# Gate matrix of the dense block made between the stages of the last block, and every gather paced by a weight unit

## The chip, the cores and the metric

The kernel runs on one core of a Trainium2 chip, as one program of five engines (PE for matmuls, DVE, ACT and POOL for the rest, SP for issuing plain transfers) that each work through their own list of instructions in order and wait for each other through semaphores. The metric is device time in microseconds; the number that counts is the median of a few runs.

## The reference, cut to what matters

One decoder layer for 1024 tokens of width 1024. Three token mixers (a state-space branch, a gated spatial branch, cross-attention to 256 memory rows) are merged and projected; then comes a channel mixer with 16384 single-neuron experts, of which each token takes 8 heads x 16.

```
def block(xt):                                   # PEER, 128 tokens
    q = (xt @ w_peer_q).reshape(t, HEADS, 2, HALF)
    sc = einsum('thid,hikd->thik', q, peer_keys)     # scores against 128 + 128 keys
    top_v, top_i = top_k(sc, 16)
    cand, cidx = sums of all pairs (i, j), index i * 128 + j
    best_v, best_pos = top_k(cand, 16); eid = cidx[best_pos]
    gate = softmax(best_v)
    act = gelu(einsum('thkd,td->thk', peer_u[eid], xt))
    return einsum('thk,thkd->td', gate * act, peer_v[eid])
x = x + peer_ffn(rms_norm(x)); return rms_norm(x)
```

## The kernel before

The tokens are handled in three blocks of 256, 512 and 256 (`BLOCKS`). Each block goes through `mixer` (projections, branches, output projection) and then `routing` (scores, top 16, gates). The mixer of a block is a generator: it hands back labels such as "conv", "chunk", "gap", "attended", and the caller puts other work at these places. So the routing of block 0 stands beside the first convolutions of block 1, and the routing of block 1 beside those of block 2; the routing of block 2 has no mixer beside it.

The expert layer is done in two ways. Blocks 0 and 2 (512 tokens, four tiles `tt` of 128) **gather**: for each of the 128 slots of a token tile, `rows_of` (L804) has POOL issue an indirect transfer of 128 rows of 4 KB from `u`; DVE multiplies it with the token rows and sums (L821, into a column of the tile `dots`); after a gelu the same is done with rows of `v`, which DVE adds up in PSUM (L828). That makes 1024 gathers of 512 KB. They land in `NG` = 7 buffers with the tags `g40` to `g46`, slot k in buffer k mod 7. The middle block (`DENSE`) computes all experts densely: `dense_act` (L943) makes an activation tile of 128 experts, a "uT" unit; `gate_matrix` (L832) writes the gates as a dense matrix to memory (`g_d`); `dense` (L865) multiplies both and runs the product through all of `v`.

A **unit** (L170) is 512 KB of weights: a load, a rounded copy `whi` by ACT (L163) and the remainder `wlo` by POOL or DVE (L164). Each product is then three matmuls (L190 to L192). 64 of the 128 activation tiles are made early and stored (`fill`, `act_d`): three at each head of the routing of block 1, two at each chunk and gap of the mixer of block 2, two at each head of its routing.

`gate_matrix` works on 4 tokens at a time, a "quad", 128 of them: two one-hot matrices by DVE (L847), a scaling by POOL (L851) and ACT (L854), four matmuls of 128x128 (L857), and a copy by ACT into a stage tile of 2 MB (L859), which is stored after every 8 quads (L861). It stands alone between the last routing and the dense stage, with 8 uT units beside it.

The order of instructions on every engine is set when the program is built, by a scheduler that goes by a priority (`tc.cur_priority`) and by its own estimate of when operands and buffers are ready. Buffers of one tag are handed out in the order in which the code asks for them, and the code of the gathers is the last to ask (L1059). `pace` gives a gather the priority of a weight unit, so that it stands behind that unit: the first ones behind units of the first routing, those from 300 (`NPRE`) on behind units of the dense stage. Between these, pace returns nothing and the scheduler places the gathers where it finds room.

## Time and profile before

| what | value |
|---|---|
| median of three runs | 3782.76 us (3782.18 to 3792.6) |
| the profiled execution | 3768.97 us, of which the span of its instructions is 3767.2 us |
| busy: PE, DVE, POOL, ACT | 87%, 77%, 67%, 39% |
| granted PE clock, mean | 0.938 |
| read and written in HBM | 953.95 MB and 72.35 MB |

All stage times below are of the profiled execution. The stages overlap at their ends, since each engine passes from one to the next by itself; the cuts used here are where DVE begins and ends a routing, and where PE begins the dense stage and DVE ends it. The share of busy time is a mean over stages with different limits.

### The profile page before, as it was taken

The page shows a single profiled execution, that of the slowest core. Times are in us where ns is not written, and L with a number is a line of the kernel's source. Part 1 is how long each engine was busy: PE and PEld are TensorE (multiplying, and loading weights), DVE is VectorE, ACT ScalarE, POOL GpSimd, SP SyncE. Part 2 cuts the span into 40 slices and gives each one's busy share as a digit, 9 for nine tenths or more (in the row PEclk, how much of TensorE's full clock was granted, in tenths as well). Part 3 has the DMA queues.
Part 4 walks back from the last instruction along what each step waited for, and adds up shares of the span by engine and source line. Part 5 has one row for each costly group of instructions (what it writes and reads, how often), then busy time and mean ns, then how long its engine had stood idle before and what let it go on. Part 6 is the DMA issues. An engine that isn't in the chain of part 4 may idle for free.

```text
span 3767.2 us, 49553 instructions
## 1 busy us (share of the span) xinstructions
PE 3292.5 (87%) x16928; PEld 2774.3 (74%) x16928; DVE 2910.4 (77%) x5391; ACT 1485.9 (39%) x2212; POOL 2527.5 (67%) x1860
## 2 busy tenths in 40 slices
PE   7899979889999888883999986488899999999995
PEld 6799867768877677763788875377777778777774
DVE  2532479998888899999741389967679988887988
ACT  5554544434223345432354443276322223222221
POOL 6577756777787666666876667655456666665665
PEclk9999999999999899986999998698999999999998
DMA  5355555789999988777965577744899999998997
GB/s 194 101 166 188 202 189 201 264 321 340 339 355 339 336 303 278 250 242 260 360 222 166 182 250 250 276 175 194 304 327 362 329 350 344 352 343 311 357 330 281
DMA packets 362653, 1029.61 MB, mean 273 GB/s; under 512 B 33568, under 2 KB 118944, under 8 KB 359968
## 3 DMA queue, kind: packets, MB, share of 16 engines
q0 software_dynamic: 147456, 536.94, 39.5%
q1 hardware_dynamic: 214944, 489.50, 37.8%
q8 instruction: 134, 2.20, 0.2%
q14 instruction: 119, 0.97, 0.1%
HBM read 953.95 MB, written 72.35 MB: 272 GB/s over the span
## 4 chain that ended last, share of the span: by engine, by line
PE 35%; DVE 22%; issue 8%; POOL 5%; ACT 3%; DMA 2%; POOLq 0%; DVEq 0%; ACTq 0%; SPq 0%
PE mm_ps L191 9%; PE mm_ps L192 9%; PE mm_ps L190 9%; DVE g L821 5%; DVE row_ps L828 3%; POOL g L811 2%; PE tp_ps L192 2%; PE tp_ps L190 2%; PE tp_ps L191 2%; POOL wlo L164 2%; PE mm_ps L857 1%; DVE d L847 1%; DVE wlo L164 1%; DMA g<-in_v_dram,eid 1%; ACT a L859 1%
## 5 line engine op out<-in xcount | busy, mean ns | idle before, releaser
L164 POOL TENSOR_TENSOR wlo<-raw,whi 128x1024 fp32r<-128x1024 f32 x484 | 1162.1, 2404 | 423.9 <-ACT whi L163 396.8
L163 ACT CAST whi<-raw 128x1024 fp32r<-128x1024 f32 (+1 forms) x623 | 648.0, 1044 | 1095.0 <-PE mm_ps L191 329.8
L190 PE MATMUL mm_ps<-a,whi 128*128 128x512 f32 (+1 forms) x2744 | 947.6, 349 | 113.6 <-ACT whi L163 42.9
L192 PE MATMUL mm_ps<-a,wlo 128*128 128x256 f32 (+1 forms) x2744 | 937.3, 344 | 33.1 <-DVE wlo L164 19.6
L191 PE MATMUL mm_ps<-a,whi 128*128 128x512 f32 (+1 forms) x2744 | 941.2, 343 | 1.1 <-DVE a L164 0.9
L811 POOL DMA_INDIRECT g<-in_v_dram,eid x512 | 537.8, 1050 | 361.8 <-DVE row_ps L828 212.2
L811 POOL DMA_INDIRECT g<-in_u_dram,eid x512 | 528.6, 1032 | 326.5 <-DVE g L821 158.4
L828 DVE SCALAR_TENSOR_TENSOR row_ps<-g,dots,row_ps 128x1024 f32<-128x1024 f32 x512 | 656.5, 1282 | 21.0 <-DMA g<-in_v_dram,eid 14.6
L190 PEld LDWEIGHTS mm_ps<-a,whi 128*128 128x128 f32 x2744 | 534.2, 195 | 182.6 <-ACT whi L163 49.6
L821 DVE SCALAR_TENSOR_TENSOR g<-g,row_ps 128x1024 f32<-128x1024 f32 x512 | 608.5, 1208 | 40.5 <-DMA g<-in_u_dram,eid 40.2
L192 PEld LDWEIGHTS mm_ps<-a,wlo 128*128 128x128 f32 x2744 | 533.2, 195 | 94.8 <-DVE wlo L164 21.6
L191 PEld LDWEIGHTS mm_ps<-a,whi 128*128 128x128 f32 x2744 | 535.4, 195 | 56.6 <-DVE a L164 2.1
L191 PE MATMUL mm_ps<-wlo,d 128*128 128x512 f32 x1024 | 410.2, 401 | 5.3 <-POOL wlo L164 4.6
L192 PE MATMUL mm_ps<-whi,d 128*128 128x512 f32 x1024 | 406.2, 399 | 0.0
L190 PE MATMUL mm_ps<-whi,d 128*128 128x512 f32 x1024 | 375.7, 399 | 20.7 <-ACT d L163 8.7
L190 PEld LDWEIGHTS mm_ps<-whi,d 128*128 128x128 f32 x1024 | 193.2, 189 | 73.1 <-ACT whi L163 9.7
L164 DVE TENSOR_TENSOR wlo<-raw,whi 128x1024 fp32r<-128x1024 f32 x139 | 194.6, 1400 | 58.0 <-ACT whi L163 57.0
L191 PEld LDWEIGHTS mm_ps<-wlo,d 128*128 128x128 f32 x1024 | 195.2, 191 | 55.9 <-POOL wlo L164 8.0
L192 PEld LDWEIGHTS mm_ps<-whi,d 128*128 128x128 f32 x1024 | 194.9, 190 | 46.5
L857 PE MATMUL mm_ps<-d,d 128*128 128x128 f32 x1024 | 156.6, 315 | 55.6 <-POOL d L851 39.4
L857 PEld LDWEIGHTS mm_ps<-d,d 128*128 128x128 f32 x1024 | 143.8, 223 | 69.0 <-POOL d L851 54.9
L847 DVE TENSOR_TENSOR d<-iota,tp_ps 128x512 bf16<-128x512 f32 (+1 forms) x256 | 155.5, 678 | 36.9 <-ACT tr L839 24.8
(311 smaller groups left out, 5052.7 us busy)
## 6 DMA issues: line engine op xcount, KB each, us to landing
raw<-in_win_a_dram SPq DMA_DIRECT2D x156, 512.0 KB, 4.2
raw<-in_uT_a_dram SPq DMA_DIRECT2D x128, 512.0 KB, 5.3
raw<-in_v_b_dram SPq DMA_DIRECT2D x128, 512.0 KB, 6.7
raw<-in_br_a_dram SPq DMA_DIRECT2D x72, 512.0 KB, 3.9
g_d<-a SPq DMA_DIRECT2D x16, 2048.0 KB, 6.3
a<-g_d SPq DMA_DIRECT2D x32, 1024.0 KB, 10.7
raw<-in_win_b_dram SPq DMA_DIRECT2D x48, 512.0 KB, 4.9
raw<-in_pq_a_dram SPq DMA_DIRECT2D x48, 512.0 KB, 3.6
```

The lines of the kernel that those rows point to most:

```text
L163: return (nc.scalar.copy(hi, src), (eng or nc.vector).tensor_tensor(lo, src, hi.bitcast(F32), op=ALU.subtract))
L164: (eng or nc.vector).tensor_tensor(lo, src, hi.bitcast(F32), op=ALU.subtract))
L190: nc.tensor.matmul(ps, lhsT=l_hi, rhs=r_hi, start=start, stop=False)
L191: nc.tensor.matmul(ps, lhsT=l_hi, rhs=r_lo, start=False, stop=False)
L192: nc.tensor.matmul(ps, lhsT=l_lo, rhs=r_hi, start=False, stop=stop)
L811: nc.gpsimd.indirect_dma_start(out=g, out_offset=None, in_=a[table], in_offset=bass.IndirectOffsetOnAxis(ap=eid[:, k:k + 1], axis=0))
L821: nc.vector.scalar_tensor_tensor(g, g, 1.0, xn, op0=ALU.mult, op1=ALU.mult, accum_out=col(w, k))
L828: nc.vector.scalar_tensor_tensor(acc, g, col(w, k), acc, op0=ALU.mult, op1=ALU.add)
L847: nc.vector.tensor_tensor(one_hot, iota[:, None, :].to_broadcast([P, 4, P]), tp[:, n * P + m0:n * P + m0 + 4, None].to_broadcast([P, 4, P] ...
L857: nc.tensor.matmul(ps[:, u * P:(u + 1) * P], lhsT=oj[:, u, :], rhs=oi[:, u, :], start=True, stop=True)
L859: nc.scalar.copy(stage[:, :, q * 4:q * 4 + 4].rearrange("p i t -> p t i"), ps.rearrange("p (t i) -> p t i", t=4))
```

## The change

The gate matrix becomes a generator that hands back after every quad. It is asked for 8 quads (one stage tile) at each "gap" of the last block's mixer, and the branches and the spatial loop get more gaps (26 in all instead of 10). Its one-hot tiles no longer come from the dense stage's pool: both f32 matrices of a quad lie in a gather buffer, one of `g44` to `g46`, and the stage tile is a `b16` buffer of the mixer. The stored activation tiles are 56 instead of 64, made at other places: 2 at each head of the routing of block 1, one at each gap once the gate matrix is done, 3 at each head of the last routing, the rest after it. `pace` now has a unit for every gather: units of the routings and mixers carry rates (`RATE_ROUTING`, `RATE_MIXER`, `RATE_LAST`), and what is left is spread over the dense units. While the gate matrix is made, gathers are to use four buffers (`slots`). 30% of the remainders of the dense stage's units go to DVE, before 50%.

```diff
-NPRE = 300
-RATE_ROUTING = 0.5
-ACT_SPILL = 64
-FILL_ROUTING = (3, 2)
-FILL_GAP = 2
+RATE_ROUTING, RATE_MIXER = (1.0, 0.3), (1.5, 0.5)
+RATE_LAST = 0.5
+ACT_SPILL = 56
+FILL_ROUTING = (2, 3)
+NQ_GATHER = 4
+QUADS_GAP = 8
-LO_MIXER, LO_DENSE = 0.34, 0.5
+LO_MIXER, LO_DENSE = 0.34, 0.3
...
-            g = gat.tile([P, D], F32, tag=f"g4{k % NG}", name="g4", bufs=1)
+            g = gat.tile([P, D], F32, tag=f"g4{k % slots(n)}", name="g4", bufs=1)
...
-            stage = a16().rearrange("p (i t) -> p i t", t=STG)
+                stage = b16().rearrange("p (i t) -> p i t", t=STG)
...
+                    quad = gat.tile([P, D], F32, tag=f"g4{NQ_GATHER + nq[0] % (NG - NQ_GATHER)}", name="quad", bufs=1)
...
-        rate[0] = 0
+        rate[0] = RATE_MIXER[b - 1]
         now = nxt
...
-            if held_xT:
-                fill(FILL_GAP)
+    m_gate = len(marks)
+    quads = gate_matrix(ij_dense, gate_dense)
+    gates_done = False
     for label in now:
         if label == "gap":
-            fill(FILL_GAP)
+            for _ in range(QUADS_GAP):
+                if next(quads, 0) == 0:
+                    gates_done = True
+            if gates_done:
+                fill(1)
+        elif label == "attended":
+            for _ in quads:
+                pass
...
+    m_gathers = len(marks)
+    rate[0] = RATE_LAST
     routing(xnT, b16()[:, 0:2048], gate[:, 2:4], eid[:, 2:4], beside=lambda: fill(FILL_ROUTING[1]))
...
-    for t in range(TT):
-        gate_matrix(t, ij_dense, gate_dense, dp, beside_gates)
+    fill(len(todo), dp)
+    acts = [dense_act(i, held_xT[0], dp, None, mm_ps()) for i in range(AHEAD)]
+    rate[0] = 0
...
-        if n < NPRE:
-            return None
-        return units[min(int((n - NPRE) * len(units) / (TT * SLOTS - NPRE)) + lag, len(units) - 1)]
+        return units[min(int((n - n1) * len(units) / (TT * SLOTS - n1)) + lag, len(units) - 1)]
+
+    def slots(n):
+
+        shared = n < n1 and m_gate <= at[bisect_right(due, n) - 1] < m_gathers
+        return NQ_GATHER if shared else NG
```

The built order of instructions shows at three places what this moves. A row names a line of its own kernel; lines of the changed kernel are up to 14 higher. First POOL in the first routing, before; the DMA rows are gathers, and consecutive slots have names three apart:

```order
L760 TENSOR_TENSOR b_4673<-b_4673,topi 128x512
L811 DMA g_27932<-in_u_dram,eid 128x1024
L811 DMA g_27935<-in_u_dram,eid 128x1024
L811 DMA g_27938<-in_u_dram,eid 128x1024
L811 DMA g_27941<-in_u_dram,eid 128x1024
L811 DMA g_27944<-in_u_dram,eid 128x1024
L811 DMA g_27947<-in_u_dram,eid 128x1024
L811 DMA g_27950<-in_u_dram,eid 128x1024
L164 TENSOR_TENSOR wlo<-raw,whi 128x1024
L811 DMA g_27953<-in_u_dram,eid 128x1024
```

The same place on POOL in the changed kernel:

```order
L769 TENSOR_TENSOR b_4673<-b_4673,topi 128x512
L820 DMA g_27648<-in_u_dram,eid 128x1024
L820 DMA g_27651<-in_u_dram,eid 128x1024
L820 DMA g_27654<-in_u_dram,eid 128x1024
L820 DMA g_27657<-in_u_dram,eid 128x1024
L165 TENSOR_TENSOR wlo<-raw,whi 128x1024
L820 DMA g_27669<-in_u_dram,eid 128x1024
L165 TENSOR_TENSOR wlo<-raw,whi 128x1024
L820 DMA g_27672<-in_u_dram,eid 128x1024
L820 DMA g_27675<-in_u_dram,eid 128x1024
L165 TENSOR_TENSOR wlo<-raw,whi 128x1024
L820 DMA g_27678<-in_u_dram,eid 128x1024
```

Slots 0 to 3 and 7 to 10 (buffers `g40` to `g43`) stand here; slots 4, 5 and 6 do not. The next gather on POOL stands in the mixer of block 2, behind the last scaling of a quad (L864):

```order
L864 TENSOR_TENSOR quad<-quad,tr 128x384 x8
L529 TENSOR_TENSOR b_10218<-b_10218,t_16541 128x256
L165 TENSOR_TENSOR wlo<-raw,whi 128x1024
L529 TENSOR_TENSOR b_10218<-b_10218,t_16576 128x256
L165 TENSOR_TENSOR wlo<-raw,whi 128x1024
L864 TENSOR_TENSOR quad<-quad,tr 128x384 x5
L820 DMA g_27666<-in_u_dram,eid 128x1024
L820 DMA g_27660<-in_u_dram,eid 128x1024
L820 DMA g_27663<-in_u_dram,eid 128x1024
```

By DVE's products with gathered rows, 4 of 1024 stand ahead of the last one-hot matrix; before, 576 stood ahead of the first. The second place is DVE at the end of the dense stage, in the kernel before (L940 is the last step of the dense stage, L828 a product with a gathered row):

```order
L828 SCALAR_TENSOR_TENSOR row_ps<-g_31061,dots,row_ps 128x1024
L940 SCALAR_TENSOR_TENSOR a_21046<-a_21046,rs_r,row 128x1024 x4
L828 SCALAR_TENSOR_TENSOR row_ps<-g_31064,dots,row_ps 128x1024
...
L828 SCALAR_TENSOR_TENSOR row_ps<-g_31091,dots,row_ps 128x1024
L148 TENSOR_SCALAR rs_v<-ssf 128x1
```

And in the changed kernel (L945 adds a dense result, L830 and L837 are the products with gathered rows):

```order
L945 TENSOR_TENSOR a_20514<-a_20514,mm_ps 128x512
L830 SCALAR_TENSOR_TENSOR g_29498,dots<-g_29498,row_ps 128x1024
...
L954 SCALAR_TENSOR_TENSOR a_20514<-a_20514,rs_r,row 128x1024 x4
L830 SCALAR_TENSOR_TENSOR g_29534,dots<-g_29534,row_ps 128x1024
...
L837 SCALAR_TENSOR_TENSOR row_ps<-g_30807,dots,row_ps 128x1024
L149 TENSOR_SCALAR rs_v<-ssf 128x1
```

Behind the last addition of a dense result stood 18 such products, and now stand 426 (45 slots of `u` and 128 of `v` for the third tile, 128 and 128 for the fourth; 3 of them wait in the pipeline). On POOL 429 gathers follow the last weight unit. The third place is ACT at the stage tile's first copy, with the semaphores that each row waits for (DMAHW is a plain transfer). Before, in the gate matrix:

```order
L859 COPY a_19412<-mm_ps 128x4x128 [waits PE_49] x2
L163 CAST whi<-raw 128x1024 [waits DMAHW2_49,PE_49]
L946 ACTIVATE d_19549<-mm_ps 128x512 [waits PE_49]
L839 COPY tr<-tp_ps 128x128 [waits PE_49]
...
L859 COPY a_19559<-mm_ps 128x4x128 [waits DMAHW7_49,PE_49]
```

And in the changed kernel, in the mixer of block 2, where L164 is the rounded copy of a weight unit:

```order
L872 COPY b_14641<-mm_ps 128x4x128 [waits PE_49]
L867 ACTIVATE quad<-quad,tr 128x128 [waits DVE_49,Pool_49]
L164 CAST whi<-raw 128x1024 [waits PE_49]
L867 ACTIVATE quad<-quad,tr 128x128 [waits DVE_49] x2
L164 CAST whi<-raw 128x1024 [waits DMAHW0_49,PE_49]
L164 CAST whi<-raw 128x1024 [waits DMAHW1_49,PE_49]
L867 ACTIVATE quad<-quad,tr 128x128 [waits DVE_49]
L872 COPY b_14807<-mm_ps 128x4x128 [waits DMAHW0_49]
```

Before, that wait is for the store of the tile before the last one (two tiles take turns). Now it is for the store of the tile just filled: one buffer serves all 16.

## Rows read from the trace of the kernel before

**Rows 1.** Windows, one for each stage; after the engines granted clock, DMA share, GB/s

```profile
0.00:484.00 484.00, 430.52 (x2931) 394.49 (x2932) 180.50 (x315) 257.38 (x419) 330.08 (x171) 0.97 0.51 168
484.00:743.00 259.00, 224.38 (x1177) 191.38 (x1176) 229.66 (x772) 119.02 (x175) 181.97 (x139) 0.93 0.65 222
743.00:1316.00 573.00, 530.22 (x2418) 426.57 (x2417) 499.17 (x655) 200.40 (x332) 433.68 (x347) 0.96 0.93 338
1316.00:1756.00 440.00, 327.88 (x1696) 280.37 (x1693) 436.54 (x1271) 178.78 (x235) 292.76 (x220) 0.86 0.78 265
1756.00:2170.00 414.00, 383.96 (x2237) 334.68 (x2238) 195.98 (x219) 187.65 (x275) 310.25 (x184) 0.97 0.69 238
2170.00:2388.00 218.00, 154.03 (x832) 133.49 (x831) 206.12 (x686) 73.25 (x105) 154.22 (x124) 0.87 0.75 254
2388.00:2674.00 286.00, 207.64 (x1252) 184.65 (x1252) 209.05 (x357) 170.97 (x279) 158.25 (x174) 0.82 0.55 210
2674.00:3731.00 1057.00, 1033.87 (x4392) 828.71 (x4392) 923.04 (x1090) 294.90 (x388) 654.57 (x493) 0.99 0.94 338
3731.00:3767.00 36.00, 0.00 (x0) 0.00 (x0) 30.34 (x37) 3.53 (x7) 11.76 (x12) 0.55 0.69 260
```

**Rows 2.** Windows of the gathers on POOL alone (L811): busy us and count

```profile
743.00:1316.00 573.00, 264.17 (x258) 0.96 0.93 338
2674.00:3731.00 1057.00, 436.74 (x403) 0.99 0.94 338
```

**Rows 3.** Windows of DVE's products, second routing: L821 (two instructions each), then L828

```profile
1316.00:1756.00 440.00, 87.08 (x146) 0.86 0.78 265
1316.00:1756.00 440.00, 82.73 (x65) 0.86 0.78 265
```

**Rows 4.** The page's line of POOL's remainders; the dense stage on its own (window as rows 1)

```profile
L164 POOL TENSOR_TENSOR wlo<-raw,whi 128x1024 fp32r<-128x1024 f32 x484 | 1162.1, 2404 | 423.9 <-ACT whi L163 396.8
...
2750.00:3650.00 900.00, 881.39 (x3751) 706.25 (x3750) 786.83 (x919) 251.24 (x323) 561.80 (x421) 0.99 0.95 340
```

**Rows 5.** The last block's mixer in two parts (windows, columns as in rows 1)

```profile
1800.00:2000.00 200.00, 184.16 (x1071) 159.23 (x1070) 112.16 (x115) 90.17 (x123) 160.21 (x101) 0.98 0.80 278
2000.00:2170.00 170.00, 165.79 (x973) 145.94 (x972) 44.37 (x63) 79.41 (x120) 113.21 (x58) 1.00 0.52 172
```

**Rows 6.** Lines of the gate matrix, ns min/median/max; its store's landing; its matmuls in order

```profile
L859 ACT COPY a<-mm_ps x128: 1023/1084/1267, 2406.2 to 2652.8; 128x512 f32<-128x512 f32 x128
L854 ACT ACTIVATE d<-d,tr x128: 377/402/470, 2402.9 to 2651.7; 128x128 f32<-128x128 bf16 x128
DMA to landing us min/median/max: 6.2/6.3/12.2
2542.12 10.85 PE L857 MATMUL mm_ps<-d,d 128*128 128x128 f32 x78 [3.79 <-POOL d L851]
```

**Rows 7.** The page: the gathers' queue, and loads of remembered keys and values

```profile
q0 software_dynamic: 147456, 536.94, 39.5%
b<-kv_d SPq DMA_DIRECT2D x2, 2048.0 KB, 10.5
```

**Rows 8.** Gathers close together: start, us; DVE, then POOL; then a window

```profile
3746.22 13.21 DVE L828 SCALAR_TENSOR_TENSOR row_ps<-g,dots,row_ps 128x1024 f32<-128x1024 f32 x10
2396.57 0.94 POOL L811 DMA_INDIRECT g<-in_u_dram,eid  x1 [0.30 <-issue]
2397.82 0.94 POOL L811 DMA_INDIRECT g<-in_u_dram,eid  x1 [0.30 <-issue]
2425.00:2435.00 10.00, 4.15 (x16) 3.56 (x16) 10.00 (x18) 2.82 (x6) 6.96 (x8) 0.50 0.95 340
```

**Rows 9.** From one token tile to the next on DVE, in the dense stage

```profile
3108.50 1.27 DVE L828 SCALAR_TENSOR_TENSOR row_ps<-g,dots,row_ps 128x1024 f32<-128x1024 f32 x1
3124.65 1.21 DVE L821 SCALAR_TENSOR_TENSOR g<-g,row_ps 128x1024 f32<-128x1024 f32 x1
```

**Rows 10.** Landing of the gathers (all 1024)

```profile
DMA to landing us min/median/max: 4.0/6.8/12.5
```

More of the change, by code (lines that the diff above doesn't have):

```diff
@@ L519, in branch @@
             for f in range(KD):
+                if f % 2:
+                    yield "gap"
                 sg = gate(n, f)
@@ L526, in branch @@
                     nc.gpsimd.tensor_tensor(merged[:, f, :], merged[:, f, :], sg, op=ALU.add)
-        branch(0, yT)
+        yield from branch(0, yT)
         ss = sml.tile([P, TT], F32, tag="ss", name="ss")
@@ L553, in mixer @@
         for g in range(8):
+            if g % 2:
+                yield "gap"
             ug, wsp = ug_next, wsp_next
@@ L568, in mixer @@
             split(yT[0][:, g, :], yT[1][:, g, :], m1)
-        branch(1, yT)
-        kv = a16() if compact else b16()
+        yield from branch(1, yT)
+        kv = b16()
         nc.sync.dma_start(kv, kv_d)
@@ L607, in turn_probs @@
         def turn_probs(prs):
-            pT = [tp_ps()[:, :T], tp_ps()[:, :T]]
+            if compact:
+                both = tp_ps()
+                pT = [both[:, 0:T], both[:, T:2 * T]]
+            else:
+                pT = [tp_ps()[:, :T], tp_ps()[:, :T]]
             for t in range(TT):
@@ L639, in mixer @@
         nc.sync.dma_start(x2, x_d[t0:t0 + T, :].rearrange("(t p) d -> p t d", p=P))
-        branch(2, yT)
+        yield from branch(2, yT)
         yield "gap"
@@ L800, in held, with gathered @@
         return ps
-    def gathered(tt, eid, gt, pace):
+    def gathered(tt, eid, gt, pace, slots):
         def rows_of(table, k, half):
@@ L1044, in layer_kernel @@
     units = marks[m_dense:m_last]
-    early_units = [m for m in marks if m[3] > 0]
+    at = [n for n, m in enumerate(marks) if m[3] > 0]
+    early_units = [marks[n] for n in at]
     due, total = [], 0.0
@@ L1054, in pace @@
             return early_units[bisect_right(due, min(n + lag * .5, due[-1])) - 1]
-        if n < NPRE:
-            return None
-        return units[min(int((n - NPRE) * len(units) / (TT * SLOTS - NPRE)) + lag, len(units) - 1)]
+        return units[min(int((n - n1) * len(units) / (TT * SLOTS - n1)) + lag, len(units) - 1)]
+    def slots(n):
+        shared = n < n1 and m_gate <= at[bisect_right(due, n) - 1] < m_gathers
+        return NQ_GATHER if shared else NG
     for t in range(TT):
-        gathered(t, eid[:, t], gate[:, t], pace)
+        gathered(t, eid[:, t], gate[:, t], pace, slots)
 _OUTS = [((1, 1024, 1024), 'float32')]
```

75 lines of the change are left out of this document (36 added, 39 removed).

## The prediction

> **What bounds the kernel now.** I read the windows cut by stage first [rows 1], since the means of the page hide that the stages have different limits. PE is the limit in the projections at the start, in both large mixers and above all in the dense stage (1033.87 of 1057 us, clock 0.99). DVE is the limit in the routings: 436.54 of 440 us in the second, 206.12 of 218 us in the third. The stage between 2388 and 2674 us, in which the gate matrix is made, has no engine over 73% busy and costs 286 us; that is what the change goes after. The gathers are filler: 258 of 1024 are issued in the mixer of block 1 and 403 in the dense stage [rows 2]. In the second routing their products cost DVE 87.08 + 82.73 = 170 of its 440 us [rows 3]. At the end, 18 products stand behind the dense stage, and the kernel ends 36 us after it.
>
> **The change: what it does to the gathers.** This decides the forecast. The quads now live in `g44` to `g46`, and they ask for these buffers earlier in the code than any gather does. A gather of slot 4, 5 or 6 therefore comes after the last quads, and the products of one tile, which all write `dots`, stand in order: after slot 3 nothing goes on. The built order shows it: 8 gathers in the first routing, none in the mixer of block 1 and the second routing, the ninth behind the last quad. The rates for these units have no effect. From there to the dense stage some 180 are issued, in the dense stage 408 (now 403), and 426 products are left behind it. An engine's order can't be changed by the chip, so this remainder is certain; only its pace is open.
>
> **Part by part.** From row to row of [rows 1], in us:
>
> 1. *Start, 484*: nothing moves, 484.
>
> 2. *First routing and mixer of block 1, 259 + 573 = 832.* 4 products with gathered rows instead of some 310 leave DVE mostly idle. PE was busy for 224.38 + 530.22 = 755, so no more than 77 can come back. DVE was not what PE waited for in the mixer (573 - 530 = 43 of idle in all, 499 busy on DVE), and in the routing DVE's own 230 - 70 remain in a chain; I take 24 off: **808** (755 to 832).
>
> 3. *Second routing, 440.* Without its gathers DVE has 436.54 - 170 = 267 left. PE has 327.88 less 8 uT units. A unit is 24 matmuls of 900 / 3751 = 0.240 us [rows 4], 5.76 us, so 8 are 46 us: 282 left. Neither engine fills such a stage alone when both are needed for each head; at the 88% that DVE and PE reach in the first routing (230 and 224 of 259) PE's 282 becomes **320** (282 to 400), 120 less.
>
> 4. *Mixer of block 2, 414.* Until 1800 nothing changes (44). The quads lie between there and some 2000. PE gains 128 x 8 matmuls of 10.85 / 78 = 0.139 us, 142 us [rows 6], and loses about 12 uT units, 69 us: 184 + 142 - 69 = 257, now 184 [rows 5]. But ACT has a floor of its own. The stage tile has one buffer, where two took turns. Each of 16 tiles needs 8 copies of 1.084, 8 scalings of 0.402 and the store's 6.3 before the next can begin [rows 6], 8.7 + 3.2 + 6.3 = 18.2, and 16 of them 291 us. Behind a copy that waits for the store stand the rounded copies of the next weight units, and PE waits for these. I take a little over that floor, 310 for the 200 (260 to 360). POOL's scaling of f32 in place is not in the trace; by its remainders, 2404 ns for 1024 f32 elements [rows 4], 384 take 0.90, 115 us in all. POOL would then have about 310 - 56 + 115 + 88 - 31 = 426 of 575 (less early gathers, plus scalings and backlog, less 13 units), so no cost; between nothing and twice that it stays under the sum. Then the backlog starts: some 85 gathers before 2170, where there were none. A gather takes the 16 DMA engines 0.395 x 3767 / 1024 = 1.45 us [rows 7], 123 us, on top of 0.52 x 170 = 88 [rows 5]: 211 for 170, so I take 213 (165 to 225), set by transfers. The keys and values of the memory need the buffer of the last stage tile and come 6.3 + 10.5 us after its filling [rows 6, 7], in part under two queries: 8 (0 to 17). Sum 44 + 310 + 213 + 8 = **575** (470 to 650).
>
> 5. *Third routing, 218.* DVE does the same with 61 gathers for 62. PE has 8 units more, 154 + 46 = 200 of 218. **226** (215 to 245).
>
> 6. *Gate stage, 286.* Left are 6 + 8 uT units, 14 x 5.76 = 81, of which a few start under the routing. **75** (60 to 105).
>
> 7. *Dense stage, 1057.* 64 activations instead of 56: 8 x 5.76 = 46, with PE at 98% and as many gathers as before. POOL does 135 remainders instead of 92, 43 x 2.40 = 103 us more on 655 [rows 1, 4], still under 72%. **1103** (1085 to 1140).
>
> The dense stage then ends at 484 + 808 + 320 + 575 + 226 + 75 + 1103 = 3591, against 3731: the moved gate matrix alone is worth 140 us.
>
> 8. *The remainder, 36 now.* 426 gathers with nothing beside them. POOL can issue one every 2397.82 - 2396.57 = 1.25 us; DVE takes 87.08 / 73 = 1.19 for a row of `u` [rows 3] and 13.21 / 10 = 1.32 for one of `v` [rows 8]. From 2425 to 2435 gathers alone moved 340 GB/s at a DMA share of 0.95 [rows 8], so 524,288 bytes each take 1.54 us; the mean over the run is 1.45. I take 1.50 (1.25 to 1.67, the last by the dearest of these with a tenth on it): 639 us. Three changes from `u` to `v` or tile to tile follow; each has 3124.65 - 3109.77 = 15 us without a product [rows 9], of which the filled buffers give back some: 12 each, 36. The last tile's norm and store need 8, as now. **683** (570 to 770).
>
> Span: 3591 + 683 = 4274. The profiled execution lies 2 us above its span and the median of the runs 14 above that; I say 4280, 13% slower.
>
> **The rivals.**
>
> *The remainder goes at DVE's pace.* If transfers keep up, 173 rows of `u` at 1.25 (POOL's pace, DVE's being shorter) and 253 of `v` at 1.32 take 550 instead of 639: about 4190. For it: 7 buffers and a median landing of 6.8 us [rows 10], taken under load, allow one gather in about 1.2 us. Against: the window at 340 GB/s had POOL issuing without a wait for DVE in most of its gathers and still did not reach that. The Trainium skill (DMA: Bandwidth & Descriptors, Anatomy of one DMA) gives a transfer from POOL 2.0 us and its bytes at 436 GB/s; by that page's figures seven in flight would never be the limit, and this rival would hold. No row here shows gathers quite alone.
>
> *The last mixer chokes.* If the single stage tile stops ACT in every one of 16 rounds for a store that takes the 12.2 us of the worst row [rows 6] instead of 6.3, that is 16 x 6 = 94 more: 4370. For it: POOL's and SP's transfers share the same 16 engines, and weights are loaded at the same time. Against: the backlog has not begun there, and DMA was at 0.80 with gathers that are now gone.
>
> *The change does what it says.* If gathers did run early and only a remainder like now's stayed, the end would be at 3591 + 36 = 3627, a good 4% **faster**. It would need gathers ahead of the quads on POOL; the order has 8. The point from which it turns: the 140 us gained before the end pay for 140 / 1.5 = some 90 gathers more in the remainder, and there are 408 more.
>
> **How the numbers follow.** Forecast 4280: 0.62. DVE's pace, 4190: 0.18. Choked mixer, 4370: 0.15. As intended, 3627: 0.04. Something that cancels out to no change: 0.01. The first three are all slower. The range takes in the terms' bounds around the forecast, not all at one end at once: for stages 2 to 7 some 80 to either side, for the remainder 90, and the two rivals lie within; 4130 to 4410. About 0.3% is what a measurement of this kernel can tell from no change: faster 0.04, same 0.01, slower 0.95.
>
> **What would show it.** Right: in the slices, 600 us or more at the end with PE at 0 and DMA near 0.95; no gather on POOL from some 550 us until the gate matrix is done; DVE half empty in the second routing, which shrinks by about 120 us; the stage tile's first copies waiting for a store; the first dense product near 2490 and the last near 3590. Wrong: gathers in the mixer of block 1; a remainder at under 1.3 us a gather; a mixer of block 2 that takes no longer than before, so that the end comes nearer to 4150.

## The result, and the profile after

The changed kernel takes 4090.66 us (4087.09 to 4092.4) where the kernel before takes 3782.47 (medians of four runs each, one more of the kernel before than above); the ratio is 1.081 [1.0795, 1.0825]. Slower was right, and the place was right: a remainder of 425 products behind the dense stage. The time is 189 us below the forecast and 39 below its range. The profiled execution has a span of 4090.7 us.

The slices of the page after (engine, then busy tenths in 40 equal slices of 102 us):

```profile
PE   7899999999999998888788999999999999000000
DVE  3532576432439985666699788887888878898889
PEclk9999999999999999999899999999999999555555
DMA  5254453234233344569977999989999998999998
GB/s 193 99 200 160 164 175 118 78 111 141 96 127 135 132 135 165 207 223 350 348 267 251 326 326 335 334 308 335 326 325 330 332 334 316 370 396 363 376 369 349
```

The last six slices are the remainder: no work on PE, its granted clock at 0.5, the DMA engines full. In the middle, from the seventh slice to the fifteenth, the reverse: DMA at 0.2 to 0.4 while PE is at 0.9. These are the stages in which the gathers used to run.

Windows of the changed kernel, cut at the same events as [rows 1] (us; PE, weight loads, DVE, ACT, POOL busy and count; granted clock, DMA share, GB/s). The starting stage now ends at 492 because I cut it at DVE's first maximum; in the kernel before that event also lies at 492.

```profile
0.00:492.00 492.00, 438.61 (x2998) 402.57 (x2999) 182.59 (x316) 259.60 (x424) 332.29 (x173) 0.97 0.48 166
492.00:690.00 198.00, 191.20 (x1033) 162.48 (x1032) 147.39 (x661) 110.20 (x149) 119.10 (x80) 0.99 0.43 151
690.00:1224.00 534.00, 522.15 (x2506) 427.32 (x2505) 201.88 (x270) 201.82 (x347) 191.28 (x96) 1.00 0.31 108
1224.00:1490.00 266.00, 255.23 (x1446) 221.99 (x1444) 263.64 (x1053) 147.02 (x192) 128.18 (x71) 0.98 0.40 136
1490.00:2043.00 553.00, 463.77 (x3062) 420.33 (x3062) 361.10 (x580) 321.70 (x520) 416.50 (x333) 0.94 0.67 247
2043.00:2280.00 237.00, 200.54 (x975) 169.04 (x974) 230.80 (x683) 81.00 (x117) 167.49 (x129) 0.91 0.79 268
2280.00:2358.00 78.00, 72.28 (x310) 58.73 (x309) 54.46 (x47) 21.90 (x31) 65.14 (x48) 0.98 0.93 330
2358.00:3481.00 1123.00, 1089.61 (x4608) 872.80 (x4608) 942.04 (x1129) 315.43 (x411) 769.48 (x552) 0.99 0.92 327
3481.00:4091.00 610.00, 0.00 (x0) 0.00 (x0) 546.39 (x623) 12.97 (x19) 393.92 (x420) 0.50 0.96 371
```

And the gathers on POOL alone (one line of the kernel, by window):

```profile
492.00:690.00 198.00, 7.78 (x8) 0.99 0.43 151
690.00:1490.00 800.00, 0.00 (x0) 0.99 0.34 118
...
3481.00:4091.00 610.00, 393.92 (x420) 0.50 0.96 371
```

Eight gathers, then none for 800 us, where [rows 2] had 258 in the mixer of block 1 alone. Stage by stage, forecast against measured: first routing and mixer of block 1, 808 (counted from 484) against 732 (from 492), which puts their end at 1292 and 1224; second routing 320 against 266; mixer of block 2, 575 against 553; third routing 226 against 237; gate stage 75 against 78; dense stage 1103 against 1123; remainder 683 against 610. So the dense stage ended at 3481 and not 3591. Three terms carry the miss: 68 us in the first, 54 in the second routing, 73 in the remainder.

### The profile page after: what moved, and what is told of

Same layout as the page of the kernel before. It is cut to its first block, busy times and chain, and to the rows that moved or that the text cites. A ratio compares the mean times of both kernels' runs of the same rounds, so it can differ in the third digit from the quotient of the medians.

```text
span 4090.7 us, 49506 instructions
## 1 busy us (share of the span) xinstructions
PE 3233.4 (79%) x16928; PEld 2735.3 (67%) x16928; DVE 2930.3 (72%) x5354; ACT 1471.6 (36%) x2201; POOL 2583.4 (63%) x1897
## 5 line engine op out<-in xcount | busy, mean ns | idle before, releaser
L165 POOL TENSOR_TENSOR wlo<-raw,whi 128x1024 fp32r<-128x1024 f32 x521 | 1258.6, 2421 | 591.0 <-ACT whi L164 536.9
L164 ACT CAST whi<-raw 128x1024 fp32r<-128x1024 f32 (+1 forms) x623 | 647.5, 1044 | 1012.0 <-PE mm_ps L193 366.9
L191 PE MATMUL mm_ps<-a,whi 128*128 128x256 f32 (+1 forms) x2808 | 946.7, 340 | 24.6 <-ACT whi L164 12.9
L192 PE MATMUL mm_ps<-a,whi 128*128 128x256 f32 (+1 forms) x2808 | 942.9, 337 | 1.0 <-DVE a L165 0.9
L820 POOL DMA_INDIRECT g<-in_u_dram,eid x512 | 509.8, 996 | 306.8 <-DVE g L830 162.4
L837 DVE SCALAR_TENSOR_TENSOR row_ps<-g,dots,row_ps 128x1024 f32<-128x1024 f32 x512 | 658.9, 1287 | 47.1 <-DMA g<-in_v_dram,eid 31.9
L820 POOL DMA_INDIRECT g<-in_v_dram,eid x512 | 509.9, 996 | 283.8 <-DVE row_ps L837 142.0
L830 DVE SCALAR_TENSOR_TENSOR g<-g,row_ps 128x1024 f32<-128x1024 f32 x512 | 610.9, 1214 | 63.3 <-DMA g<-in_u_dram,eid 49.0
L191 PEld LDWEIGHTS mm_ps<-a,whi 128*128 128x128 f32 x2808 | 539.7, 193 | 82.6 <-ACT whi L164 16.2
L192 PEld LDWEIGHTS mm_ps<-a,whi 128*128 128x128 f32 x2808 | 540.9, 193 | 53.3 <-DVE a L165 1.6
L165 DVE TENSOR_TENSOR wlo<-raw,whi 128x1024 fp32r<-128x1024 f32 (+1 forms) x102 | 151.6, 1486 | 116.3 <-ACT whi L164 111.5
L191 PE MATMUL tp_ps<-a,whi 128*128 128x512 f32 x512 | 200.9, 392 | 5.5 <-ACT whi L164 5.5
L193 PE MATMUL tp_ps<-a,wlo 128*128 128x512 f32 x512 | 201.3, 393 | 2.0 <-POOL wlo L165 2.0
L192 PE MATMUL tp_ps<-a,whi 128*128 128x512 f32 x512 | 200.6, 392 | 0.0
```

Of the source, the lines that this page charges most:

```text
L164: return (nc.scalar.copy(hi, src), (eng or nc.vector).tensor_tensor(lo, src, hi.bitcast(F32), op=ALU.subtract))
L165: (eng or nc.vector).tensor_tensor(lo, src, hi.bitcast(F32), op=ALU.subtract))
L191: nc.tensor.matmul(ps, lhsT=l_hi, rhs=r_hi, start=start, stop=False)
L192: nc.tensor.matmul(ps, lhsT=l_hi, rhs=r_lo, start=False, stop=False)
L193: nc.tensor.matmul(ps, lhsT=l_lo, rhs=r_hi, start=False, stop=stop)
L820: nc.gpsimd.indirect_dma_start(out=g, out_offset=None, in_=a[table], in_offset=bass.IndirectOffsetOnAxis(ap=eid[:, k:k + 1], axis=0))
```

## The experiments

Theory: gathers stop because the quads ask first for buffers that later slots need; the remainder is the bill. Rivals: the pacing behind weight units holds them back, or the remainder is only an effect of a slower middle. Three further questions are about sizes: why the middle was so much shorter, what sets the remainder's pace, and what sets the 310 us of the quads (from the first one-hot matrix to the last, on DVE).

Runs 3 and 4 were measured five and four times, all others once. How much a stage varies without a change in it can be seen in runs 6 to 8, which differ from the changed kernel in the remainder alone: there the quads took 311, 317 and 314 us where the changed kernel has 310, and the dense stage 1114 to 1116 where it has 1123. Smaller differences are not read as effects.

**1. Four buffers until the last mixer ends.** The gathers keep out of the quads' buffers; the pacing is untouched.

```diff
-        shared = n < n1 and m_gate <= at[bisect_right(due, n) - 1] < m_gathers
+        shared = n < n1 and at[bisect_right(due, n) - 1] < m_gathers
```

> The changed kernel, with the gathers using four buffers (g40 to g43) in all units up to the end of the last mixer, not only while the gate matrix is made. Theory (gathers are held because the quads ask for g44 to g46 first): the gathers now start in the first routing and run through the mixer of block 1, 260 of them. There they stop again, since the last step of token tile 0 asks for g46 (its result tile), behind the quads. So some 200 products stay behind the dense stage instead of 425: at 1.40 us 315 us less there, some 60 us more in the first routing and mixer (DVE busy again), in all about 3840 us. Rival (the pacing rates alone put the gathers late): no gather before the quads, 4090 us as now.

Measured 3836.92. 64 gathers ran in the first routing and 196 in the mixer of block 1; then they stopped again, because the result tile of the first token tile asks for a buffer of the quads (`fin` in `g46`). 199 products stood behind the dense stage, which was followed by 287 us instead of 610. One line on buffers takes 254 us off, with the pacing as it was: it is the buffers that hold the gathers, and not the pacing.

**2. The result tile in the fourth buffer too.** As run 1, and:

```diff
-        out = gat.tile([P, D], F32, tag=f"g4{NG - 1}", name="fin", bufs=1)
+        out = gat.tile([P, D], F32, tag=f"g4{NQ_GATHER - 1}", name="fin", bufs=1)
```

> The changed kernel; until the last mixer's end the gathers use four buffers that no quad asks for, as in the run e1, and the result tile of the products sits in the fourth of them instead of one that the quads hold. Nothing is left out. The order then has 51 gathers in the first routing, 219 in the mixer of block 1, 72 in the second routing and 121 behind the dense stage (e1: 64, 196, 0 and about 193). Theory, a gather in the second routing costs DVE's 1.18 us, one in the mixer of block 1 some 0.15, one in the remainder 1.37: 78 fewer in the remainder give back 107, 72 in the second routing cost 85, 23 more in the mixer 3: about 3815 (3800 to 3825) against 3837 of e1. Rival, a gather taken out of the remainder is all gain: about 3735.

Measured 3836.41, the same as run 1, though 75 fewer products were left. The remainder took 178 us, 109 less, as expected. The second routing took 342 instead of 265 us with its 57 gathers, the mixer of block 1 597 instead of 583. Missing from both theories was what happened among the quads: 43 gathers stand there, where run 1 has none, and the stretch took 380 instead of 316 us, 1.5 us for each gather. From the quads to the end of the dense stage 48 us came back; no run was made on that. The window of the quads in run 2 (columns as above):

```profile
1724.00:2104.00 380.00, 297.76 (x1944) 277.86 (x1944) 263.60 (x410) 230.40 (x356) 261.39 (x234) 0.86 0.60 218
```

**3. Gathers asked for ahead of the quads, in all seven buffers.** The gathers' function becomes a generator that is driven up to the gate matrix's place in the code, so that the early gathers get their buffers first.

```diff
         for k in range(SLOTS):
+            yield tt * SLOTS + k / 2
             g, m1 = rows_of("u", k, 0)
...
         for k in range(SLOTS):
+            yield tt * SLOTS + (SLOTS + k) / 2
             g, _ = rows_of("v", k, 1)
...
     m_gate = len(marks)
+    so_far, prio = sum(m[3] for m in marks) - 2, tc.cur_priority
+    for n in asked:
+        if n >= so_far:
+            break
+    tc.cur_priority = prio
     quads = gate_matrix(ij_dense, gate_dense)
...
```

> The changed kernel, with the gathers whose units lie ahead of the gate matrix asked for in the code ahead of the quads (344 of them), with all seven buffers; rates, quads and everything else stay. Theory: with the order of the requests put right the gathers flow as the rates say, 480 ahead of the dense stage, 121 behind its last unit (the built order). Stages: 492 + 790 + 290 + 560 + 237 + 70 + 1123 = 3562, then 121 x 1.38 + 25 = 192: about 3755 us, no more than 1% from the kernel before. The clock in the second routing falls below 0.98, as DVE fills up. Rival (something else in the change costs the time, such as the single stage buffer or the added gaps): it stays above 3950 us.

Measured 3769.19 (3768.57 to 3772.55), ratio 0.9958 [0.9944, 0.9973]: a little faster than before, and 14 slower than expected. The gathers run where the change meant them to (81, 230 and 37 in the first three stages behind the start), and 121 products are left.

**4. The same, with more gathers in the routings.** As run 3, and:

```diff
-RATE_ROUTING, RATE_MIXER = (1.0, 0.3), (1.5, 0.5)
-RATE_LAST = 0.5
+RATE_ROUTING, RATE_MIXER = (1.0, 1.0), (1.5, 0.5)
+RATE_LAST = 1.5
```

> As the kernel with the gathers asked for early, with two rates raised (second routing 1.0 instead of 0.3, last routing and what follows 1.5 instead of 0.5), so that 5 gathers instead of 121 stand behind the last unit. Theory: the remainder goes, and the second routing takes some 70 gathers more, whose products cost DVE about 85 us there, half of it seen: 492 + 790 + 330 + 560 + 245 + 80 + 1123 + 30 = 3650 us, 3.5% faster than the kernel before. Rival (the remainder's time only moves ahead, since DVE and the transfers are full wherever PE is): 3740 us, like the one with the old rates.

Measured 3734.61 (3723.72 to 3742.13), ratio 0.9854 [0.9826, 0.9882]: better than both kernels, yet the rival held: the remainder's time moved ahead. The second routing in run 1, run 3 and run 4:

```profile
1341.00:1606.00 265.00, 254.58 (x1440) 221.44 (x1439) 263.21 (x1056) 147.40 (x191) 128.23 (x71) 0.98 0.42 137
```

```profile
1345.00:1657.00 312.00, 270.21 (x1496) 234.16 (x1493) 310.79 (x1143) 152.12 (x209) 175.95 (x114) 0.93 0.54 184
```

```profile
1352.00:1756.00 404.00, 282.20 (x1498) 243.37 (x1497) 401.21 (x1255) 158.86 (x212) 249.05 (x192) 0.84 0.72 246
```

DVE fills the stage in all three, with 0, 37 and 116 gathers: from run 3 to run 4 92 us for 79 gathers, 1.16 each, which is DVE's price. The same way a gather's price follows in each place: in the first routing 1.19 (198 to 285 us for 73 more), in the mixer of block 1 0.14 (534 to 567 for 230; with four buffers, in run 2, 0.28), among the quads 1.5, in the remainder 1.33 to 1.40. Only the mixer of block 1 is cheap, and no run of the changed kernel got more than 230 into it; the kernel before has 258 there [rows 2].

**5. The kernel before with thin products.** DVE's products with gathered rows work on 128 of 1024 columns (the rest of each sum is left out); POOL and the transfers stay.

```diff
-            nc.vector.scalar_tensor_tensor(g, g, 1.0, xn, op0=ALU.mult, op1=ALU.mult, accum_out=col(w, k))
+            nc.vector.scalar_tensor_tensor(g[:, :128], g[:, :128], 1.0, xn[:, :128], op0=ALU.mult, op1=ALU.mult, accum_out=col(w, k))
...
-            nc.vector.scalar_tensor_tensor(acc, g, col(w, k), acc, op0=ALU.mult, op1=ALU.add)
+            nc.vector.scalar_tensor_tensor(acc[:, :128], g[:, :128], col(w, k), acc[:, :128], op0=ALU.mult, op1=ALU.add)
```

> The kernel before, with the products of the gathered rows cut to 128 of 1024 columns on DVE (the result leaves out the rest); transfers and their issue on POOL stay. It asks why the early stages of the changed kernel became shorter than PE's busy time of before. Theory (DVE's products make PE wait, PE's clock falls for it, and both come back when DVE is free): first routing and mixer of block 1 go from 824 to 730 to 760 us, the second routing from 440 to 270 to 300, its granted clock from 0.86 to 0.97 or more; PE's busy time in it falls from 328 to about 290. Rival (the gathers' transfers, which share the queues with the weights, or their issue on POOL make PE wait): the mixer of block 1 stays above 560 us and the second routing above 380.

Measured 3579.01. The first routing, the mixer of block 1 and the second routing (columns as in the windows after):

```profile
493.00:716.00 223.00, 204.69 (x1089) 173.73 (x1087) 169.44 (x755) 114.72 (x168) 170.18 (x131) 0.96 0.71 247
716.00:1265.00 549.00, 525.23 (x2445) 426.46 (x2446) 282.51 (x636) 195.42 (x330) 423.43 (x336) 0.98 0.92 339
1265.00:1581.00 316.00, 296.60 (x1629) 255.04 (x1627) 295.45 (x1250) 164.77 (x213) 247.67 (x183) 0.99 0.87 313
```

With a DMA share of 0.92 in the mixer and 0.87 in the second routing, the stages are 223 + 549 = 772 us and 316 us long, 12 and 16 over what was expected and far from the rival's 380 in the second routing. There DVE's products had set the length, not the transfers. In the mixer of block 1 it is less clear: 549 us is only just under the rival's 560. PE was idle there for 43 of 573 us before, is for 24 in run 5 and for 12 of 534 in the changed kernel, so DVE's products account for some 19 us; the other 12 came back only where transfers and POOL's issues were gone as well, and these two aren't told apart.

PE's busy time for a matmul fell in the second routing from 327.88 / 1696 = 193 ns [rows 1] to 296.60 / 1629 = 182, with the clock from 0.86 to 0.99. It isn't a matter of which matmuls are counted: the commonest kind (one of the three products of a unit, 128x512, as often in both) reads in the kernel before and in run 5, in the second routing (busy us and mean ns of one, then PE's idle time before it and what ended it):

```profile
L190 PE MATMUL mm_ps<-a,whi 128*128 128x512 f32 x296 | 125.4, 424 | 33.1 <-ACT t L324 18.3 <-ACT sp L946 8.0 <-DVE t L307 6.8
...
L190 PE MATMUL mm_ps<-a,whi 128*128 128x512 f32 x296 | 117.5, 397 | 3.4 <-DVE b L721 3.1 <-ACT t L324 0.3
```

**6. Thin products in the remainder.** Products on 512 of 1024 columns there (the rest is left out), transfers whole. The slots in the text of runs 6 to 8 are those of the pacing, two gathers to a slot: "from 320 on" is `v` of the third tile and all of the fourth. The 41 rows of `u` that are left of the third tile stay as they were, so the 173 rows of `u` in the expectations of runs 6 and 7 are 128.

```diff
-            nc.vector.scalar_tensor_tensor(g, g, 1.0, xn, op0=ALU.mult, op1=ALU.mult, accum_out=col(w, k))
+            c = D // 2 if tt * SLOTS + k / 2 > 319 else D
+            nc.vector.scalar_tensor_tensor(g[:, :c], g[:, :c], 1.0, xn[:, :c], op0=ALU.mult, op1=ALU.mult, accum_out=col(w, k))
...
-            nc.vector.scalar_tensor_tensor(acc, g, col(w, k), acc, op0=ALU.mult, op1=ALU.add)
+            c = D // 2 if tt > 1 else D
+            nc.vector.scalar_tensor_tensor(acc[:, :c], g[:, :c], col(w, k), acc[:, :c], op0=ALU.mult, op1=ALU.add)
```

> The changed kernel; of the gathers of slots 320 on (third tile's second half and fourth tile), the products with u, and all products with v of the last two tiles, work on 512 of the 1024 columns (the rest of the sum is left out). The transfers and POOL's issues stay as they are. In the changed kernel the remainder runs at 1.38 us for a row of u and 1.33 for a row of v. Theory, the transfers set the remainder's pace: 1.38 and 1.33 stay, within 0.03, and the end stays at about 4085 (4070 to 4092). Rival, DVE's products set it: they halve to about 0.65 us, so the next limit is POOL's issue at 1.25; v falls by 0.08 on 253 rows and u by 0.13 on 173, some 40 us in all, to 4050 or less.

Measured 4076.41, 14 less than the changed kernel. In the two profiles, which lie 16 us apart, 9 us are the remainder's (601 for 610), and the rest lies ahead of it, where nothing was changed. The end lies in the theory's bounds, but the paces say otherwise. From product to product (first to last of a tile's 128, on DVE) `v` fell from 1.33 to 1.27 and 1.28: DVE had set it. `u` did not fall: 1.37 before, 1.41 now. Windows that are mostly `v` of the third tile, `u` of the fourth and `v` of the fourth, in the changed kernel:

```profile
3545.00:3730.00 185.00, 0.00 (x0) 0.00 (x0) 169.59 (x138) 4.90 (x6) 120.96 (x129) 0.50 0.97 374
3730.00:3915.00 185.00, 0.00 (x0) 0.00 (x0) 157.27 (x258) 1.22 (x2) 120.54 (x130) 0.50 0.97 368
3915.00:4080.00 165.00, 0.00 (x0) 0.00 (x0) 160.57 (x125) 0.00 (x0) 112.71 (x120) 0.50 0.98 384
```

and in run 6, the last line well inside `v` of the third tile:

```profile
3545.00:3730.00 185.00, 0.00 (x0) 0.00 (x0) 102.88 (x156) 4.90 (x6) 124.75 (x134) 0.50 0.99 388
3730.00:3915.00 185.00, 0.00 (x0) 0.00 (x0) 88.52 (x242) 1.22 (x2) 120.99 (x130) 0.50 0.96 362
3550.00:3695.00 145.00, 0.00 (x0) 0.00 (x0) 84.69 (x113) 0.00 (x0) 106.22 (x114) 0.50 1.03 409
```

In `v` DVE is at 160.57 of 165 in the changed kernel (last window); in run 6 it is at little over half, and the transfers gain 14 GB/s in the window of `v`, none in that of `u`. Inside `v` they now reach 409 GB/s at a DMA share of 1.03, one gather in 1.28 us: they are the next limit, close behind DVE's 1.33.

**7. Half rows in the remainder.** Each gather fetches 512 of 1024 columns from slot 320 on (other data than the reference uses); products with `u` on 512 columns, those with `v` as two operations of 512.

```diff
-                nc.gpsimd.indirect_dma_start(out=g, out_offset=None, in_=a[table],
+                nc.gpsimd.indirect_dma_start(out=g[:, :c], out_offset=None,
+                                             in_=a[table] if c == D else a[table].rearrange("n (h c) -> (n h) c", h=2),
...
+            for o in range(0, D, c):
+                nc.vector.scalar_tensor_tensor(acc[:, o:o + c], g[:, :c], col(w, k), acc[:, o:o + c], op0=ALU.mult, op1=ALU.add)
```

> The changed kernel; from slot 320 on each gather fetches half a row (512 of 1024 columns, so other data than the reference uses), the products with u work on 512 columns, and the products with v are two operations of 512 columns each, so that DVE's time for v stays near 1.3 us. Half of the remainder's bytes are left out. Theory, the transfers set the remainder's pace: u and v both fall to the next limit, 1.25 us (POOL's issue) for u and at most 1.32 (DVE) for v, so 173 rows of u win 0.13 each, 22 us, the v rows 3 or less: end at about 4065. Rival, DVE sets the pace of v and POOL that of u: v stays at 1.33 and u at 1.38, end at 4085. If v falls below 1.3, both were wrong and two half products are cheaper than one whole one.

Measured 4151.72, which neither theory had. `v` went to 1.58: two half products cost more than a whole one, so for `v` the run tells nothing of transfers. `u` of the fourth tile is a clean reading: half the bytes, half the product, and 1.36 a gather as before. The windows of `v` and of `u`:

```profile
3545.00:3730.00 185.00, 0.00 (x0) 0.00 (x0) 176.66 (x235) 0.00 (x0) 109.86 (x117) 0.50 0.56 163
3730.00:3915.00 185.00, 0.00 (x0) 0.00 (x0) 100.90 (x265) 4.90 (x6) 118.00 (x125) 0.50 0.64 185
```

DVE is full in the first (176.66 of 185, 0.75 for a half product); in the second neither DVE nor the DMA engines are, and the pace stays. So bytes don't set the mean pace of `u`.

**8. Five buffers in the remainder.**

```diff
-            g = gat.tile([P, D], F32, tag=f"g4{k % slots(n)}", name="g4", bufs=1)
+            g = gat.tile([P, D], F32, tag=f"g4{k % (slots(n) if n <= 319 else NQ_GATHER + 1)}", name="g4", bufs=1)
```

> The changed kernel; from slot 320 on the gathers take turns in five buffers instead of seven; nothing is left out. In the remainder POOL issues u at a mean of 1.46 us (median 1.25, with pauses of 2.1 in bunches) and v at 1.40 (median 1.33), and products on half the columns changed only v (median 1.25). Theory, for u the round through the buffers is the limit, some 7 x 1.46 = 10 us from an issue to the next in the same buffer: with five, u goes to about 2.0 us, v to between 1.6 and 2.0, and the end to about 4260 (4180 to 4320). Rival, the pauses come from elsewhere and a buffer is back in under 5 x 1.25 us: the paces stay, end 4080 to 4110.

Measured 4145.37: between the two. `u` went to 1.51 and `v` to 1.54 and 1.55, a round of 5 x 1.53 = 7.7 us. Five buffers hold the pace back. By that round seven would allow 7.7 / 7 = 1.1, an estimate that takes the round to be no longer with seven in flight; so with seven the ring is probably not what sets the pace on average. What remains of `u` are pauses that come in bunches. POOL in the changed kernel, start, duration, what it waited for:

```profile
3802.04 0.94 POOL L820 DMA_INDIRECT g<-in_u_dram,eid  x1 [0.39 <-DVE g L830]
3803.46 0.94 POOL L820 DMA_INDIRECT g<-in_u_dram,eid  x1 [0.48 <-DVE g L830]
3805.55 0.94 POOL L820 DMA_INDIRECT g<-in_u_dram,eid  x1 [1.16 <-DVE g L830]
3807.66 0.94 POOL L820 DMA_INDIRECT g<-in_u_dram,eid  x1 [1.17 <-DVE g L830]
3808.90 0.94 POOL L820 DMA_INDIRECT g<-in_u_dram,eid  x1 [0.30 <-DVE g L830]
3810.14 0.94 POOL L820 DMA_INDIRECT g<-in_u_dram,eid  x1 [0.30 <-issue]
```

Some ten gathers come at POOL's 1.25, then a few late ones, two of them here at 2.1, each released by a semaphore of DVE. But DVE wasn't late with its work: by its timeline the product that had last read the buffer ended at 3803.25 for the gather of 3805.55, and at 3804.53 for that of 3807.66. The pauses are there with thin products and with half rows too. Why POOL is released so late in these places stays open.

**9. A small store of the stage tile.** Each store writes the first 512 of 4096 columns of a partition, and the dense stage reads only those (the rest of the gate matrix is left out).

```diff
-                        nc.sync.dma_start(g_d[t * (P // STG) + s], stage.rearrange("p i t -> p (i t)"))
+                        nc.sync.dma_start(g_d[t * (P // STG) + s, :, 0:512], stage.rearrange("p i t -> p (i t)")[:, 0:512])
...
-                nc.sync.dma_start(gb[:, g % 2], g_d[:, :, g * GCH * STG:(g + 1) * GCH * STG].rearrange("q p c -> p q c"))
+                g4 = g % 4
+                nc.sync.dma_start(gb[:, g % 2], g_d[:, :, g4 * GCH * STG:(g4 + 1) * GCH * STG].rearrange("q p c -> p q c"))
```

> The changed kernel; each store of a stage tile of the gate matrix writes the first 512 of 4096 columns of a partition (256 KB instead of 2 MB), and the dense stage reads only those (the rest of the matrix is left out). The quads take 310 us in the changed kernel. Theory of the prediction, ACT with the wait for the single stage tile's store is the floor (16 x 18.2 = 291): a store of 256 KB lands in some 2.5 us instead of 6.3, so 16 x 3.8 = 61 go and the stretch falls to 250 to 270, where PE's own 257 take over; end near 4040. Rival, the stretch is ACT's and PE's own work with weight units between the quads and the store is hidden: the stretch stays at 300 or more, and the end within 10 of 4090.

Measured 4067.18, but not by the quads: their stretch stayed, 308 for 310 us. The gain lies elsewhere (dense stage 1101 for 1123, mixer of block 2 543 for 553). For the quads the rival holds: the store is hidden. The end, 23 us earlier, lies outside the rival's 10; why the dense stage got shorter was not tested (it now reads the same 512 columns over and over, as many bytes as before).

**10. Two scalings on POOL instead of three.**

```diff
-POOL_G = 3
+POOL_G = 2
```

> The changed kernel with two of the four scalings of a quad on POOL and two on ACT, instead of three and one; nothing is left out. In the 310 us of the quads PE is busy for 269 us and idle for 41, 31 of it until POOL has scaled a quad. Theory, POOL's scaling is what PE misses: POOL has some 0.28 us less in each of 128 quads, 35 in all, ACT 0.41 more, 52 on 222 of 310; PE's waits for POOL shrink by half or more and the stretch falls to 285 to 300. Rival, ACT: its 274 of 310 then hold up the rounded copies of the weight units and the stretch grows to 315 or more. Third, the one-hot matrices of DVE with the weight units between them set it: 305 to 315 as now.

Measured 4110.98, 20 slower; the stretch went to 335 us. The quads in the changed kernel, in run 9 and in run 10:

```profile
1517.00:1827.00 310.00, 269.06 (x1945) 249.94 (x1943) 200.23 (x329) 222.04 (x352) 217.99 (x190) 0.97 0.52 191
```

```profile
1519.00:1827.00 308.00, 269.99 (x1950) 251.60 (x1950) 201.27 (x330) 221.12 (x353) 218.08 (x190) 0.96 0.31 104
```

```profile
1518.00:1853.00 335.00, 285.52 (x1952) 264.53 (x1951) 201.14 (x331) 257.80 (x479) 190.32 (x190) 0.92 0.49 178
```

Run 9 lowers the DMA share from 0.52 to 0.31 and the stretch stays. Run 10 loads ACT with 36 us more and takes 28 from POOL, and the stretch grows by 25, far more than the 310 to 317 us that it varies by otherwise. The theory fails: PE's waits for POOL stay at 30.8 us, where they were 31.4. ACT's rival held (315 or more); that it is ACT's own work that counts is argued from the size, and the rounded copies that it names were not looked at one by one.

## Why the prediction was wrong, step by step

**The mechanism and the sign were right.** The order told which products would be left, and 425 of the 426 were. Run 1 shows it with one line on buffers. The rival "the change does what it says" (3627) is missed even where the gathers do run early: runs 3 and 4 end at 3769 and 3735, since that rival let them run for nothing.

**Step 2 failed: "PE was busy for 224.38 + 530.22 = 755, so no more than 77 can come back."** 92 came back: the mixer of block 1 ended at 1224 instead of 1316. Busy time is no floor where the clock is not full. With the first cut at 492, as after, the first routing of the kernel before reads

```profile
492.00:743.00 251.00, 216.38 (x1110) 183.38 (x1109) 229.12 (x771) 116.90 (x171) 180.05 (x138) 0.93 0.66 226
```

and with the mixer of [rows 1] that is 747 us of PE for 3528 matmuls, 212 ns each, at clocks of 0.93 and 0.96. The changed kernel has 191.20 + 522.15 = 713 us for 3539, 202 ns each, at 0.99 and 1.00. Of the 92 us, 33 are PE's own busy time that shrank; the other 59 are idle time, which went from 77 to 19. So the forecast itself, 24 us back, failed twice: it left PE's busy time as it was, and it gave back too little of the idle time because "DVE was not what PE waited for in the mixer". Run 5 shows that in part it was: with thin products alone 19 of the mixer's 43 idle us came back.

**Step 3 failed the same way: "282 left", then 320.** The stage took 266, and PE was busy for 255.23 at 0.98: 1446 matmuls of 177 ns, where it had 1696 of 193 at 0.86. So PE's time fell by 73 us, where 46 were subtracted for the 8 units; the 27 in between put the lower bound of 282 above the truth. Not all of 193 to 177 is the clock: the units that left cost 240 ns a matmul, and by that figure the mean without them would have been 187 before. The clean figure is run 5's, 182 for 193 with the same program on PE. The 88% of the first routing, by which 282 became 320, was also read in a stage that DVE held up; without the gathers PE is busy for 96% and DVE for 99% of this one. What bounds the stage is DVE's 263.64 us, close to the 267 that the forecast had left it and then passed over; of the 54 us missed, the larger part is that 88%. The sign "DVE half empty in the second routing" was wrong by the same reading. How the clock falls can be seen in the kernel before, in 8 us windows of the second routing (columns as above):

```profile
1612.00:1620.00 8.00, 4.74 (x38) 4.33 (x36) 8.00 (x29) 2.27 (x4) 6.29 (x5) 1.00 0.73 218
1620.00:1628.00 8.00, 1.67 (x4) 1.38 (x5) 8.00 (x21) 1.54 (x2) 7.64 (x6) 0.61 0.71 220
1628.00:1636.00 8.00, 8.00 (x28) 6.31 (x28) 8.00 (x30) 4.69 (x6) 3.24 (x5) 0.74 0.83 289
1636.00:1644.00 8.00, 8.00 (x38) 6.58 (x37) 8.00 (x19) 3.98 (x6) 6.62 (x5) 1.00 0.72 231
1644.00:1652.00 8.00, 8.00 (x41) 6.76 (x40) 8.00 (x23) 3.86 (x5) 5.25 (x5) 1.00 1.00 388
```

DVE is full all along. PE runs out of work (4.74, then 1.67 us busy): it waits 7.5 us for an operation of ACT, which itself waited 4.7 us for a step of the routing on DVE. The clock drops between its two levels of 2.4 and 1.2 GHz to a mean of 0.61, and when work comes PE is busy for all of the third window and does 28 matmuls at 0.74, where the next window has 38 at 1.00, 36 of them of the same shape. The third window counts as fully busy, and holds a quarter fewer matmuls. Run 5 shows it apart from the change: thinner products on DVE alone, and a matmul on PE took 182 ns instead of 193. The Trainium skill (Perfetto Trace Analysis, Identifying the Most-Contended Engine) says that matmul busy share is not a good measure of how near PE is to its limit; its reason is pipelining, the reason here is the clock, and this case's rows agree with the rule.

**Step 4: the sum was nearly right (575 for 553), and its reason was not.** The quads took 310 us, as forecast. But the floor that I gave, 16 rounds of copies, scalings and a store of 6.3 us = 291, does not exist: with a store of an eighth the stretch stays (run 9). Nor do the waits of the changed kernel in that stretch show one, though a sign named in the prediction was the first copies waiting for a store (engine and line, what it waited for, us, times, longest):

```profile
POOL quad L864 <- DVE quad L860: 51.5, 75, 4.1
...
PE mm_ps L870 <- POOL quad L864: 31.4, 19, 4.1
...
ACT b L872 <- DMA g_d<-b: 8.6, 8, 2.7
```

The copies waited 8.6 us in all for a store, the matmuls 31.4 for POOL. ACT does matter, by its own 222 us of work and by what queues behind it (run 10), and PE is at 269 of 310. That the number fitted was luck. The backlog part took 216 us at a DMA share of 0.94, as forecast (213).

**Steps 5 to 7** were off by 11, 3 and 20 us. In the dense stage 1089.61 of 1123 is PE's, 56 more than before, where 46 were counted.

**Step 8 was mis-sized: 1.50 us a gather, measured 1.33 for `v` and 1.37 for `u`** (the part of `u` in the third tile 1.39). For some 422 steps from product to product, 422 x (1.50 - 1.35) = 63 of the 73 us; most of the rest is the changes from `u` to `v` or tile to tile, 8.6 to 10.3 us without a product instead of 12. The source of 1.50 was "340 GB/s at a DMA share of 0.95" from a 10 us window of the kernel before, taken as a cap. It was not one: alone, the gathers move 368 to 384 GB/s in the windows of the changed kernel, and inside `v` of run 6 409. So the rival "DVE's pace" was nearly right on the remainder: it gave 594, measured 610. For `v` DVE sets the pace, as it said; for `u` it is POOL's 1.25 plus pauses whose cause is open. Its price of 4190 missed mainly because it stood on the same steps 2 and 3: with the dense stage's end at 3481 it gives 4075, 16 under what was measured. By the Trainium skill's figures in that rival (DMA: Bandwidth & Descriptors, Anatomy of one DMA: 2.0 us and 436 GB/s, by which 512 KB take an estimated 1.20 us beyond the fixed part) transfers would not be the limit. For `v` the trace agrees, 1.33 being DVE's price, though with 1.28 measured in run 6 it is a near thing; for `u` half the bytes changed nothing (run 7).

**The range** was too narrow for a reason that can be named. Its lower ends of steps 2 and 3 (755, 282) were called bounds and were readings at a lowered clock; both were broken, by 15 (484 + 755 = 1239 against 1224) and by 16 us. Steps 2, 3 and 8 were off in one direction, and the first two in part by one cause, so their errors added where the range had let them cancel. There is also a slip at the end: 4274 plus the 2 and 14 us that the prediction names is 4290, and it says 4280.

## What to carry to other kernels

Before PE's busy time is taken as a floor, read its granted clock in the same window: where that is below 1, the busy time itself shrinks once the waits go, here by 5% at 0.95 (212 to 202 ns a matmul in the first routing and the mixer of block 1) and by 6% at 0.86 (193 to 182, run 5). A ring of buffers belongs to whoever asks first in the code, so a filler that shares it must be asked for ahead of the work that holds it (run 3), or keep to buffers of its own (run 1). And filler is only worth moving to a stage where a gather costs less than where it stood, which is to be measured for each stage; room on its own engine is not enough (among the quads DVE is busy for 200 of 310 us, and a gather still cost 1.5). Here 304 gathers fewer in the remainder gave 321 us (run 3), most of it by way of the cheap mixer, and the next 116 gave 35 (run 4).

## What was new about the hardware

- Gathers with almost nothing beside them (rows of 4 KB, 512 KB each) moved 371 GB/s over the whole remainder at a DMA share of 0.96, and 409 inside `v` of run 6 at 1.03, where the dense stage has 327 at 0.92.
- A product of DVE on 1024 columns (`v`) took 1.29 us and one on 512 columns 0.755: two halves cost 1.51, 17% more than a whole (from gather to gather 1.58 for 1.33).
- POOL's gathers left at the earliest every 1.24 to 1.25 us, with whole rows and with half rows alike.
